# Sixteen-head gated DeltaNet trunk: the 32x32 products of the chunk inverses issued in turns instead of loop by loop

## The chip, the cores and the metric

The kernel runs on one core of one Trainium2 chip. The metric is the device time of one execution in microseconds (us); the value of a kernel is the median over its runs.

## The reference, cut to what matters

A two-layer decoder trunk over 512 tokens of width 1024: a gated DeltaNet mixer, a gated MLP with a causal convolution, sliding-window attention on a shared K/V, a second gated MLP, and a final norm. All inputs and outputs are float32. The change lies in the mixer, in what the reference writes as a triangular solve per chunk and head:

```python
m = jnp.where(strict, jnp.einsum('bnhcd,bnhsd->bnhcs', k_beta, k) * decay, 0.0)
t_mat = lax.linalg.triangular_solve(m + eye, eye, left_side=True, lower=True,
                                    unit_diagonal=True)
u = jnp.einsum('bnhcs,bnhse->bnhce', t_mat, v_beta)
w = jnp.einsum('bnhcs,bnhsd->bnhcd', t_mat, k_beta * jnp.exp(gc)[..., None])
```

`t_mat` is the inverse of a unit lower triangular matrix. The reference has chunks of 64 tokens; the kernel works with chunks of 128, which gives the same output, so each inverse is 128x128. There are 4 chunks and 16 heads, 64 inverses.

## The kernel before, in words

The mixer works in four groups of four heads. Projections run with the weights as the stationary operand: each weight block is split on ACT (`whi`, line 129) and DVE (`wlo`, line 130) into two parts, and `mm3` (lines 145 to 147) makes three matmuls of 128x128 by 128x512 per block. These "large matmuls" fill most of PE's (TensorE's) time. Their results lie in PSUM banks with the tag `d`. There are further banks with the tags `g` (two), `s` (two) and `p` (one).

A chunk's inverse is built in three steps:

- `solve` (lines 498 to 526) inverts the four 32x32 blocks on the diagonal of all 16 inverses of a group at once on DVE, by forward substitution, and sends them through DRAM into `Xg`, where they lie on the diagonal.
- `levels(g, pr)` (from line 529) fills in what is below the diagonal. It is called twice in each group, for pair 0 and pair 1 (two heads, four chunks each: 8 inverses). It first takes a transposed copy `sy` (DVE, line 532), and then has two levels. The first joins 32x32 blocks into 64x64 ones: a first stage of 32x32 products (lines 539 and 541) from `Xg` and the matrix `nt` into the banks `s` and `p`; two copies into `pz` (ACT, lines 544 and 545); and a second stage of 32x32 products (lines 548, 552 and 556) from `pz` and `sy`, read by DVE (lines 560 to 562). The second level joins 64x64 blocks: line 565, a copy on ACT (569), line 572, and DVE (580).
- `scan(g, c)` runs the recurrence over the four chunks and uses the inverses (line 610). Its output goes to DRAM (`od`), and `gate(h)` reads it back (line 674, SP's queue), scales it (ACT, 678), transposes it (PE, 681), multiplies it by the gate (DVE, 682) and stores it to `yd` (683). The output projection reads `yd` back (773), and loads and transposes `x` (784, 787).

A 32x32 product uses one 32x32 sub-array of the 128x128 array: its rows are the partitions of the operands, its columns the partitions of the result. The five loops and their sub-arrays (rows / columns): line 539, rows 0 to 31 / columns 32 to 63; line 541, 64 to 95 / 96 to 127; line 548, 32 to 63 / 32 to 63; line 552, 32 to 63 / 0 to 31; line 556, 96 to 127 / 64 to 95. Each loop makes 8 products on one and the same sub-array. A float32 product appears in the trace as two matmuls (and two weight loads).

The order of the work isn't the order of the code. The jobs of the mixer are listed in the table `ORDER`, where L0 and L1 are the two calls of `levels`, C0 to C3 the scans, `z` and `g` the gate's projections and products, and P, Q, V, K other jobs of this or the next group. Each job gets a priority from its place, and a scheduler then orders every instruction on each engine by priority and by when its inputs and its buffer are free, by its own estimate of times. So an edit in one place can move instructions elsewhere. Each engine works through its queue in order, and SP's queue issues nearly all transfers.

Of the kernel before, what the change touches and what calls it, by code (L numbers as in the profile page):

```python
# [41 lines left out]
def kernel(  # L42
# [27 lines left out]
    V, S, G, PE, SP = nc.vector, nc.scalar, nc.gpsimd, nc.tensor, nc.sync  # L70
# [36 lines left out]
    def pair(tag, dt=F32):  # L107
        return main.tile([P, 2, T], dt, tag=tag, bufs=PAIRS[tag], name=nm(tag))

    def bank(tag):  # L110
        return psum.tile([P, T], F32, tag=tag, bufs=BANKS[tag], name=nm(tag))
# [417 lines left out]
    def levels(g, pr):  # L529
        Yt = pair("sy")  # L530
        X = Xg[:, 2 * pr : 2 * pr + 2, :]
        V.transpose(Yt[:].rearrange("p h t -> p (h t)"), X.rearrange("p h t -> p (h t)"))
        y4 = Yt[:].rearrange("p h (n j) -> p (h n) j", n=NC)
        x4 = X.rearrange("p h (n j) -> p (h n) j", n=NC)
        n4 = st[g]["nt", pr][:].rearrange("p h (n j) -> p (h n) j", n=NC)
        z = pz[pr]
        p1, p2 = bank("s"), bank("p")
        for c in range(8):
            PE.matmul(p1[32:64, 32 * c : 32 * c + 32], n4[0:32, c, 32:64], x4[0:32, c, 0:32], start=True, stop=True)
        for c in range(8):  # L540
            PE.matmul(
                p2[96:128, 32 * c : 32 * c + 32], n4[64:96, c, 96:128], x4[64:96, c, 64:96], start=True, stop=True
            )
        S.copy(z[32:64, :], p1[32:64, 0:256])
        S.copy(z[96:128, :], p2[96:128, 0:256])
        p3, p4 = bank("s"), bank("p")
        for c in range(8):
            PE.matmul(
                p3[32:64, 32 * c : 32 * c + 32], y4[32:64, c, 32:64], z[32:64, 32 * c : 32 * c + 32], start=True, stop=True
            )  # L550
        for c in range(8):
            PE.matmul(
                p3[0:32, 32 * c : 32 * c + 32], z[32:64, 32 * c : 32 * c + 32], y4[32:64, c, 32:64], start=True, stop=True
            )
        for c in range(8):
            PE.matmul(
                p4[64:96, 32 * c : 32 * c + 32], z[96:128, 32 * c : 32 * c + 32], y4[96:128, c, 96:128], start=True, stop=True
            )
        blocks = lambda ps, r: ps[r : r + 32, 0:256].rearrange("p (n j) -> p n j", n=8)
        V.tensor_scalar(x4[32:64, :, 0:32], blocks(p3, 32), -1.0, None, op0=ALU.mult)  # L560
        V.tensor_scalar(y4[0:32, :, 32:64], blocks(p3, 0), -1.0, None, op0=ALU.mult)
        V.tensor_scalar(y4[64:96, :, 96:128], blocks(p4, 64), -1.0, None, op0=ALU.mult)
        p6 = bank("p")
        for c in range(8):
            PE.matmul(
                p6[64:128, 64 * c : 64 * c + 64], n4[0:64, c, 64:128], x4[0:64, c, 0:64], start=True, stop=True
            )
        p6s = tmp6
        S.copy(p6s[64:128, :], p6[64:128, :])
        p7 = bank("s")  # L570
        for c in range(8):
            PE.matmul(
                p7[0:64, 64 * c : 64 * c + 64],
                p6s[64:128, 64 * c : 64 * c + 64],
                y4[64:128, c, 64:128],
                start=True,
                stop=True,
            )
        yb = y4[0:64, :, 64:128]
        V.tensor_tensor(yb, yb, p7[0:64, :].rearrange("p (n j) -> p n j", n=8), op=ALU.subtract)  # L580
        st[g]["y", 2 * pr], st[g]["y", 2 * pr + 1] = Yt[:, 0, :], Yt[:, 1, :]
        G.memset(x4[32:64, :, 0:32], 0.0)
# [108 lines left out]
    def bias_rows():  # L691
# [20 lines left out]
        "T": key_tokens,  # L712
        "V": value_proj,
        "L": levels,
        "C": scan,
        "B": key_norms,
# [566 lines left out]
```

## Time and profile before

| what | value |
|---|---|
| median of 3 runs | 1455.04 us |
| the three runs | 1465.84, 1454.49, 1455.04 us |
| the profiled execution | 1461.97 us |
| its span (first to last instruction) | 1460.2 us |
| PE busy | 1424.7 us (98%) |
| mean granted clock of PE | 0.989 |
| the eight calls of `levels` | between 129.8 and 434.2 us |
| matmuls of each of the five 32x32 loops | 128 (8 calls x 8 products x 2) |
| first matmul of the output projection, ahead of the mixer's last scans | 441.1 us |

Durations of single matmuls overlap: PE starts one while others run, so the distance from start to start, not the duration, is what one costs. Times in the views are from the span's start. In the timeline, neighbouring instructions of one line are merged into one piece with a count; where two lines alternate, the pieces are single instructions. In the rows of stretches the columns are: stretch, length, PE busy and number of matmuls, granted clock, share of the DMA engines, GB/s.

### The profile page before, as it was taken

How to read it: one execution, taken by the hardware profiler on the slowest of the kernel's cores; microseconds unless marked ns; L12 is line 12 of the kernel's file. 1: busy time of each engine (PE TensorE's matmuls, PEld its weight loads, DVE VectorE, ACT ScalarE, POOL GpSimd, SP SyncE). 2: the span in 40 equal slices, each digit the busy share in tenths (PEclk: the TensorE clock that was granted, in tenths of full speed). 3: DMA queues.
4: the chain of work that ended last, by engine and by line, in shares of the span. 5: the costliest groups of instructions: out<-in, count | busy, mean ns of one | idle time of the engine just before them, and what ended most of it. 6: DMA issues, size and time to landing. Idle time of an engine off the chain costs nothing.

```text
span 1460.2 us, 21604 instructions
## 1 busy us (share of the span) xinstructions
PE 1424.7 (98%) x8266; PEld 1188.8 (81%) x8266; DVE 1118.9 (77%) x2048; ACT 769.7 (53%) x1510; POOL 20.0 (1%) x47
## 2 busy tenths in 40 slices
PE   7999999999999999999999999899999999999998
PEld 5778888888887788888988889777788888988887
DVE  4896885976945446888978899878667889977896
ACT  7764564655646424444434445668745444444443
POOL 1000000000000000000000000100000000000000
PEclk9999999998999999999999999999999999999999
DMA  5334253162356533231242223231033321342222
GB/s 154 83 108 111 75 175 114 62 188 73 123 163 219 161 115 108 87 116 44 96 151 87 87 60 115 87 101 51 30 114 110 99 81 60 116 137 87 94 66 79
DMA packets 163084, 152.85 MB, mean 105 GB/s; under 512 B 24164, under 2 KB 150693, under 8 KB 162981
## 3 DMA queue, kind: packets, MB, share of 16 engines
q1 hardware_dynamic: 160722, 151.27, 32.7%
q8 instruction: 65, 1.06, 0.3%
q10 hardware_dynamic: 2259, 0.20, 0.2%
q14 instruction: 38, 0.31, 0.1%
HBM read 134.65 MB, written 16.80 MB: 104 GB/s over the span
## 4 chain that ended last, share of the span: by engine, by line
PE 87%; DVE 6%; DMA 4%; ACT 2%; issue 1%; DVEq 0%; ACTq 0%; SPq 0%
PE d L145 21%; PE d L147 21%; PE d L146 21%; DVE wlo L130 2%; PE s L595 2%; PE p L1198 1%; PE s L610 1%; PE d L999 1%; PE g L1193 1%; PE s L635 1%; PE s L999 1%; PE d L997 1%; PE d L998 1%; PE s L997 1%; PE s L998 1%
## 5 line engine op out<-in xcount | busy, mean ns | idle before, releaser
L145 PE MATMUL d<-xh,whi 128*128 128x512 f32 x1192 | 476.4, 400 | 3.7 <-ACT whi L129 3.6
L147 PE MATMUL d<-xh,wlo 128*128 128x512 f32 x1192 | 475.3, 400 | 0.5 <-DVE wlo L130 0.5
L146 PE MATMUL d<-xl,whi 128*128 128x512 f32 x1192 | 474.2, 398 | 0.0
L129 ACT CAST whi<-stage 128x1024 fp32r<-128x1024 f32 (+2 forms) x236 | 229.2, 976 | 245.5 <-PE d L146 162.6
L130 DVE TENSOR_TENSOR wlo<-stage,whi 128x1024 fp32r<-128x1024 f32 (+2 forms) x236 | 265.7, 1129 | 70.2 <-ACT whi L129 69.3
L145 PEld LDWEIGHTS d<-xh,whi 128*128 128x128 f32 x1192 | 225.4, 189 | 52.1 <-ACT whi L129 4.2
L147 PEld LDWEIGHTS d<-xh,wlo 128*128 128x128 f32 x1192 | 225.5, 189 | 51.0 <-DVE wlo L130 1.4
L146 PEld LDWEIGHTS d<-xl,whi 128*128 128x128 f32 x1192 | 225.5, 189 | 48.0 <-issue 1.0
L237 DVE SCALAR_TENSOR_TENSOR acc<-d,cwc,acc 128x511 f32<-128x511 f32 (+2 forms) x96 | 70.6, 738 | 9.1 <-ACT acc L234 8.7
L858 DVE TENSOR_TENSOR sz<-d,p6s 128x512 f32<-128x512 f32 x58 | 39.9, 688 | 40.7 <-PE d L147 38.5
L880 ACT ACTIVATE dt<-dt 128x512 f32<-128x512 f32 x44 | 27.8, 632 | 82.1 <-DVE dt L863 82.1
L863 DVE SCALAR_TENSOR_TENSOR va<-sz,fcw,va 128x511 f32<-128x511 f32 (+1 forms) x58 | 43.3, 747 | 1.8 <-ACT va L861 0.9
L863 DVE SCALAR_TENSOR_TENSOR dt<-sz,fcw,dt 128x511 f32<-128x511 f32 (+1 forms) x58 | 43.3, 746 | 0.9
L517 DVE TENSOR_TENSOR sT<-sT,p6s 64x31 f32<-64x31 f32 (+15 forms) x124 | 40.8, 329 | 1.9
L511 DVE TENSOR_TENSOR p6s<-sN,sT 64x31 f32<-64x31 f32 (+15 forms) x124 | 40.8, 329 | 1.8
L129 ACT CAST whi<-st 128x768 fp32r<-128x768 f32 (+1 forms) x30 | 23.7, 791 | 29.8 <-PE g L999 6.8
L858 DVE TENSOR_TENSOR zl<-d,p6s 128x512 f32<-128x512 f32 x30 | 20.7, 689 | 23.4 <-PE d L147 22.7
L1181 ACT ACTIVATE dt<-dt,sm 128x256 f32<-128x256 f32 (+1 forms) x64 | 30.3, 473 | 6.7 <-DVE sm L1177 6.6
L882 DVE TENSOR_TENSOR va<-dt,va 128x512 f32<-128x512 f32 x44 | 30.4, 690 | 1.2
L643 ACT ACTIVATE rq<-o 128x128 f32<-128x128 f32 x64 | 19.0, 298 | 18.0 <-DVE o L638 12.4
L130 DVE TENSOR_TENSOR wlo<-st,whi 128x768 fp32r<-128x768 f32 (+1 forms) x30 | 26.8, 899 | 1.8 <-ACT whi L129 1.7
L861 ACT ACTIVATE dt<-sz,normc,fcw 128x512 f32<-128x512 f32 x29 | 23.7, 817 | 5.2 <-DVE sz L858 5.1
(745 smaller groups left out, 2814.1 us busy)
## 6 DMA issues: line engine op xcount, KB each, us to landing
stage<-in_ffn_w_up_dram SPq DMA_DIRECT2D x44, 1024.0 KB, 5.2
stage<-in_a_w_in_dram SPq DMA_DIRECT2D x23, 1024.0 KB, 5.5
stage<-in_ffn_w_down_dram SPq DMA_DIRECT2D x16, 768.0 KB, 4.6
stage<-in_a_w_out_dram SPq DMA_DIRECT2D x8, 1024.0 KB, 5.1
st<-in_ffn_w_down_dram SPq DMA_DIRECT2D x8, 768.0 KB, 5.7
zd<-sz SPq DMA_DIRECT2D x16, 256.0 KB, 2.0
od<-o SPq DMA_DIRECT2D x16, 256.0 KB, 2.6
stage<-in_b_w_q_dram SPq DMA_DIRECT2D x4, 1024.0 KB, 5.1
```

The source lines that it names most:

```text
L129: S.copy(hi[:, :kt, :m], src)
L130: V.tensor_tensor(lo[:, :kt, :m], src, hi[:, :kt, :m].bitcast(F32), op=ALU.subtract)
L145: PE.matmul(ps, hi[:, k, :m], xh[k], start=first and k == 0, stop=False)
L146: PE.matmul(ps, hi[:, k, :m], xl[k][:], start=False, stop=False)
L147: PE.matmul(ps, lo[:, k, :m], xh[k], start=False, stop=last and k == kt - 1)
L237: V.scalar_tensor_tensor(acc[:, d:], ps[:, : T - d], col, acc[:, d:], op0=ALU.mult, op1=ALU.add)
L511: V.tensor_tensor(tv, N[:, s, s + 1 : 32].unsqueeze(2).to_broadcast([64, n, m]), Tm[:, s : s + 1, 0:m].to_broadcast([64, n, m]), op=ALU.mult,)
L517: V.tensor_tensor(Tm[:, s + 1 : 32, 0:m], Tm[:, s + 1 : 32, 0:m], tv, op=ALU.subtract)
L858: V.tensor_tensor(u[:], ps[:], rs[:], op=ALU.mult)
L863: V.scalar_tensor_tensor(acc[:, d:], u[:, : T - d], tap(2 - d, t), acc[:, d:], op0=ALU.mult, op1=ALU.add)
L882: V.tensor_tensor(b[:], a[:], b[:], op=ALU.mult)
L1181: S.activation(e3[:, j, :], e3[:, j, :], AF.Exp, bias=ngm[:, j : j + 1], accum_out=den[:, j : j + 1])
```

## The change

Both loops of the first stage become one loop in which the two products of a chunk follow each other, and the three loops of the second stage become one loop with the products in the order 548, 556, 552 of the old numbering. The operands, the sub-arrays, the banks and the number of products stay as they are.

```diff
         p1, p2 = bank("s"), bank("p")
         for c in range(8):
             PE.matmul(p1[32:64, 32 * c : 32 * c + 32], n4[0:32, c, 32:64], x4[0:32, c, 0:32], start=True, stop=True)
-        for c in range(8):
             PE.matmul(
                 p2[96:128, 32 * c : 32 * c + 32], n4[64:96, c, 96:128], x4[64:96, c, 64:96], start=True, stop=True
             )
...
         p3, p4 = bank("s"), bank("p")
         for c in range(8):
-            PE.matmul(
-                p3[32:64, 32 * c : 32 * c + 32], y4[32:64, c, 32:64], z[32:64, 32 * c : 32 * c + 32], start=True, stop=True
-            )
-        for c in range(8):
-            PE.matmul(
-                p3[0:32, 32 * c : 32 * c + 32], z[32:64, 32 * c : 32 * c + 32], y4[32:64, c, 32:64], start=True, stop=True
-            )
-        for c in range(8):
-            PE.matmul(
-                p4[64:96, 32 * c : 32 * c + 32], z[96:128, 32 * c : 32 * c + 32], y4[96:128, c, 96:128], start=True, stop=True
-            )
+            ks = slice(32 * c, 32 * c + 32)
+            PE.matmul(p3[32:64, ks], y4[32:64, c, 32:64], z[32:64, ks], start=True, stop=True)
+            PE.matmul(p4[64:96, ks], z[96:128, ks], y4[96:128, c, 96:128], start=True, stop=True)
+            PE.matmul(p3[0:32, ks], z[32:64, ks], y4[32:64, c, 32:64], start=True, stop=True)
```

The line numbers of the changed kernel differ: old line 541 is 540, the copies 544 and 545 are 543 and 544, the second stage is 548 (as before), 549 (old 556) and 550 (old 552), and every later line is 8 lower (565 is 557, 674 is 666). Here is how the scheduler places the matmuls of the first call of `levels` that follow the copies, on PE. Before:

```order
L147 MATMUL d_1724<-xh_132,wlo_1726 128x512
L548 MATMUL s_907<-pz_343,sy_885 32x32 x8
L552 MATMUL s_907<-sy_885,pz_343 32x32 x8
L556 MATMUL p_908<-sy_885,pz_343 32x32 x8
L451 MATMUL g_1488<-ident_80,qT_1415 128x128
```

In these rows stand the line, the instruction, the tile that it writes, the tiles that it reads, the shape, and how often in a row. Now:

```order
L145 MATMUL d_1724<-xh_132,whi_1725 128x512
L146 MATMUL d_1724<-xl_133,whi_1725 128x512
L147 MATMUL d_1724<-xh_132,wlo_1726 128x512
L548 MATMUL s_907<-pz_343,sy_885 32x32
L549 MATMUL p_908<-sy_885,pz_343 32x32
L550 MATMUL s_907<-sy_885,pz_343 32x32
```

The last three rows come eight times. In the whole program the first stage is merged in this way in the four calls for pair 1; in the four calls for pair 0 the loops of lines 539 and 540 stand apart, with other work between them, as before. The order of the other engines' queues is the same as before in groups 0 and 1 and drifts in places in groups 2 and 3. On PE it drifts between the two stages of the last call (group 3, pair 1). Before, with L681 the gate's transposes:

```order
L541 MATMUL p_4002<-Xg,nt_3416 32x32 x8
L147 MATMUL d_4403<-xh_132,wlo_4405 128x512
L681 MATMUL g_4124<-ident_80,ol_4116 128x128
L145 MATMUL d_4403<-xh_141,whi_4404 128x512
L681 MATMUL g_4124<-ident_80,ol_4116 128x128
L146 MATMUL d_4403<-xl_142,whi_4404 128x512
L681 MATMUL g_4124<-ident_80,ol_4116 128x128
L147 MATMUL d_4403<-xh_141,wlo_4405 128x512
L681 MATMUL g_4124<-ident_80,ol_4116 128x128
L548 MATMUL s_4021<-pz_344,sy_3999 32x32 x8
```

and now

```order
L539 MATMUL s_4001<-Xg,nt_3416 32x32
L540 MATMUL p_4002<-Xg,nt_3416 32x32
L146 MATMUL d_4403<-xl_160,whi_4404 128x512
L147 MATMUL d_4403<-xh_159,wlo_4405 128x512
L548 MATMUL s_4021<-pz_344,sy_3999 32x32
L550 MATMUL s_4021<-sy_3999,pz_344 32x32
```

The transposes now stand before this call's products, and two large matmuls are left between its stages. In the calls for pair 1 of groups 0, 1 and 3 the copies of the two results come one after the other, and the scheduler starts the second stage with seven products of lines 548 and 550 before the first of line 549. At the mixer's end the order drifts on SP: before,

```order
L773 DMA zl_4536<-yd 128x512
L674 DMA dt_4322<-od 128x4x128
L674 DMA dt_4435<-od 128x4x128
L674 DMA dt_4450<-od 128x4x128
L674 DMA dt_4465<-od 128x4x128
L119 DMA stage_4749<-in_a_w_out_dram 128x8x256
```

and now

```order
L636 DMA od<-o_4276 128x512
L119 DMA stage_4749<-in_a_w_out_dram 128x8x256
L666 DMA dt_4322<-od 128x4x128
L666 DMA dt_4435<-od 128x4x128
L666 DMA dt_4450<-od 128x4x128
L666 DMA dt_4465<-od 128x4x128
```

`stage_4749` is a block of the output projection's weights, `dt_4322` to `dt_4465` are the scan's results for the last four heads, and `od<-o_4276` is the store that they read. The weights' load now stands ahead of these reads.

## The prediction

> **What bounds the kernel now.** I read the page first, then the waits of the matmul engine, then the timeline around the lines that change.
>
> ```profile
> span 1460.2 us, 21604 instructions
> PE 1424.7 (98%) x8266; PEld 1188.8 (81%) x8266; DVE 1118.9 (77%) x2048; ACT 769.7 (53%) x1510; POOL 20.0 (1%) x47
> PE 87%; DVE 6%; DMA 4%; ACT 2%; issue 1%; DVEq 0%; ACTq 0%; SPq 0%
> ```
>
> PE is busy for 98% of the span and carries 87% of the chain that ended last. So a change on PE is worth what it takes out of PE's own sequence, plus what it does to PE's few waits. In the mixer the long ones are these:
>
> ```profile
> PE g L787 <- DVE va L682: 2.8, 1, 2.8
> PE g L324 <- DVE sz L292: 2.6, 1, 2.6
> PE s L595 <- DVE S L621: 0.8, 1, 0.8
> ```
>
> No wait at a 32x32 product is among them. What those products cost is in PE's timeline; here is one second stage (three loops of eight products, group 3, pair 1). Columns: start, duration of the piece, line, count. A float32 product is two matmuls here, so a loop of eight shows as 16.
>
> ```profile
> 427.35 0.59 PE L548 MATMUL s<-pz,sy 32*32 32x32 f32 x13
> 427.75 0.21 PE L552 MATMUL s<-sy,pz 32*32 32x32 f32 x1
> 427.78 0.19 PE L548 MATMUL s<-pz,sy 32*32 32x32 f32 x1
> 427.84 0.19 PE L552 MATMUL s<-sy,pz 32*32 32x32 f32 x1
> 427.84 0.19 PE L548 MATMUL s<-pz,sy 32*32 32x32 f32 x1
> 427.87 0.48 PE L552 MATMUL s<-sy,pz 32*32 32x32 f32 x10
> 428.16 0.21 PE L556 MATMUL p<-sy,pz 32*32 32x32 f32 x1
> 428.28 0.57 PE L556 MATMUL p<-sy,pz 32*32 32x32 f32 x13
> 428.78 0.50 PE L145 MATMUL d<-xh,whi 128*128 128x512 f32 x1
> ```
>
> Two rates stand in it. One sub-array (rows by columns of the array) takes a matmul every (0.57 - 0.19)/12 = 31.7 ns. But the next loop, on another sub-array, starts 0.40 or 0.41 us after the one before: 16 x 25.3 ns, while three matmuls of the old loop are still to start (the L548 rows at 427.78 and 427.84 follow the first L552). So PE hands out a matmul every 25.3 ns, the sub-array falls behind by 6.4 ns each time, and the next sub-array isn't held up. Already today only the **last** loop of a run pays for the lag.
>
> **The change part by part.** Nothing is added or removed: the same 40 products per call, eight calls. In the rows of PE shown with the change, the three sub-arrays now take turns, where before each had its eight products in a row. This holds for all eight second stages and for the first stage of pair 1 in each group; the first stage of pair 0 (four of eight) stays in two loops far apart, since the scheduler places its halves by when their PSUM banks come free.
>
> *Second stages.* Before, the last matmul starts at 428.28 + 0.57 - 0.19 = 428.66, 1.31 us after the first. Taking turns each sub-array has three slots, 76 ns, per matmul, so none lags, and PE's hand-out sets the pace: 47 x 25.3 ns = 1.19 us. Saved 0.12 us, eight times: 0.96 us. *Merged first stages:* two loops, the last start at 16 x 25.3 + 0.021 + 15 x 31.7 = 0.90 us (0.021 for the longer first step), now 31 x 25.3 = 0.78 us: 0.12 us, four times: 0.48 us. Together **-1.4 us**. No row shows PE alternating for long, so this has bounds. Below: nothing gained, if the turns cost 2.5 ns each. Above: 25.3 ns is no limit and each sub-array runs at its own 31.7 ns, a rival below.
>
> *What waits for these products.* A merged run ends both its results at its own end, so the first of them comes later. The readers:
>
> ```profile
> 425.46 0.36 ACT L544 COPY pz<-s 32x256 f32<-32x256 f32 x1 [0.40 <-PE s L539]
> 425.87 0.36 ACT L545 COPY pz<-p 32x256 f32<-32x256 f32 x1
> ```
>
> ```profile
> 428.48 0.42 DVE L560 TENSOR_SCALAR Xg<-s 32x256 f32<-32x256 f32 x1 [2.95 <-PE s L552]
> 429.37 0.42 DVE L562 TENSOR_SCALAR sy<-p 32x256 f32<-32x256 f32 x1
> ```
>
> ```profile
> 424.74 0.59 PE L539 MATMUL s<-Xg,nt 32*32 32x32 f32 x13
> 430.37 1.14 PE L565 MATMUL p<-Xg,nt 64*64 64x64 f32 x16
> ```
>
> ```profile
> 236.21 0.50 PE L145 MATMUL d<-xh,whi 128*128 128x512 f32 x1
> 236.87 0.59 PE L548 MATMUL s<-pz,sy 32*32 32x32 f32 x13
> ```
>
> The first stage starts at 424.74. Merged, it ends 0.78 + 0.19 = 0.97 us later, so the two copies run from 1.01 to 1.37 and from 1.41 to 1.78. Where only two large matmuls stand between the stages (236.21 to 236.87, 0.66 us, in group 1), the next stage starts at 0.78 + 0.12 + 0.66 = 1.56: after the copy that L548 needs, before the end of the one that L549 needs. There the order puts seven products (0.35 us) ahead of the first L549, which makes it 1.91. Slack 0.13 us; without it the price is some 0.2 us, four times. On DVE, L560 moves from 1.13 to about 1.39 us after the second stage's start, and L562's end from 2.44 to 2.70; L565, which needs both, started 3.02 after. Other matmuls fill PE in between. I cost both moves at **nothing**, at worst 1 us together.
>
> *What the scheduler moves besides.* Queues of groups 0 and 1 keep their order but for the merged products. In groups 2 and 3 the order drifts. Between the stages in group 3, pair 1, seven rows stood before (three large matmuls and four gate transposes L681). The transposes have moved forward, and two large matmuls are left. In group 2 two became four. At the mixer's end, in SP's queue, the megabyte of weights (`stage_4749`) now goes ahead of the four reads of `dt`. That touches the chain that ends in the longest mixer wait:
>
> ```profile
> 458.94 3.05 DMA od<-o
> 462.06 3.21 DMA dt<-od
> 467.98 7.55 DMA yd<-va
> 475.54 2.60 DMA va<-zd
> 479.07 0.66 PE g L787 x4
> ```
>
> ```profile
> 466.30 0.39 SPq L119 DMA_DIRECT2D stage<-in_a_w_out_dram  x1
> ```
>
> ```profile
> yd<-zl SPq DMA_DIRECT2D x12, 256.0 KB, 3.2
> stage<-in_a_w_out_dram SPq DMA_DIRECT2D x8, 1024.0 KB, 5.1
> ```
>
> The store of `yd` took 7.55 us where its kind takes 3.2: it ran beside the weight load issued at 466.30. Now the load sits beside the reads of `dt` instead: these land at most 5.1 us later, less what of the load has moved before the first read, and the store takes up to 4.35 us less. PE's order has 65 large matmuls and 16 transposes between the last scan product and L787, now 67 and 16, which is 0.5 us more cover for the 2.84 us wait. Bounds: the whole wait goes (-2.8), or the reads lose more than the store gains (+2). I take **-1.3 us**, nearer the row with the longer overrun, since part of the load is over before the first read is issued.
>
> *Sum.*
>
> ```profile
> 234.13:237.54 3.41, 3.41 (x75) 1.00 0.12 19
> 237.54:244.37 6.83, 6.83 (x51) 0.50 0.70 202
> 329.70:333.12 3.42, 3.42 (x77) 1.00 0.27 77
> 333.12:343.36 10.24, 10.24 (x62) 0.50 0.12 19
> ```
>
> ```profile
> 240.22 0.63 PE L147 MATMUL d<-xh,wlo 128*128 128x512 f32 x1
> 240.64 0.63 PE L145 MATMUL d<-xh,whi 128*128 128x512 f32 x1
> 431.78 0.40 PE L146 MATMUL d<-xl,whi 128*128 128x512 f32 x1
> 432.02 0.39 PE L147 MATMUL d<-xh,wlo 128*128 128x512 f32 x1
> ```
>
> The profiled execution took 1461.97 us, the median of the runs shown is 1455.04. The difference has a place (stretch, length, PE busy and count, granted clock): after the small products of groups 1 and 2 the clock falls to half for 17.07 us. A large matmul then steps 0.42 to 0.43 us instead of 0.23, so about 17.07 x 0.46 = 7.9 us are lost, and 1461.97 - 7.9 = 1454.1 is what a run without these stretches should take; 1454.49 and 1455.04 are such runs by that reckoning. The terms come off either: 1461.97 - 1.4 - 1.3 = 1459.3 with the stretches, 1455.04 - 2.7 = **1452.3** without. I forecast the latter, as the median before was of that kind.
>
> **The rivals.**
>
> *The turns run side by side.* If 25.3 ns is no limit, all sub-arrays advance at 31.7 ns at once: a run of three ends after 15 x 31.7 = 0.48 us instead of 1.31, a run of two after 0.48 instead of 0.90. 8 x 0.83 + 4 x 0.42 = 8.3 us, and with the tail 1455.04 - 8.3 - 1.3 = 1445.4. For it: matmuls of two loops do overlap at each change. Against it: all three loops start exactly 25.3 ns x 16 apart, however long their queue is. The Trainium skill, TensorE: Matmul & The Clock Gate, section "Part 3: Packing small matmuls — row/col tiling", says of matmuls in different tiles that their starts lie about 4 ns apart; by it the sum would be this rival's. The same page, in the section "Wait — 56ns, not 53.3ns?", has a floor of about 25 ns from start to start; the trace agrees with that one, with 25.3, and by it the sum is my forecast.
>
> *Half clock in the median run.* Each stretch follows some 4 us with hardly any large matmul. The change shortens these by 0.24 us and gives group 2 more large matmuls, but makes such a place in group 3. If two stretches fall into the median run, it is 1452.3 + 7.9 = 1460.2. For it: the profiled execution has them. Against: two of the three timed runs, by the sum above, have not.
>
> *Every change of sub-array drains the array: slower.* Merging makes some 21 more changes in each of eight runs and 14 in each of four, 224 in all. Between the last L556 (428.66) and the large L145 (428.78) stand 0.12 us, 0.09 more than a step of 31.7 ns. At that price each: 224 x 0.09 = 20.2 us, 1455.04 + 20.2 - 1.3 = 1473.9. It decides from about 0.07 us per change. Against it: the changes from L548 to L552 to L556 go to another column and to another row of the array, and cost no gap. The Trainium skill, TensorEngine Tiling (Array Packing), section "Key Properties", has the drain when the tiling mode changes, not the tile; the trace agrees, with 0.12 us at the change of shape and none between the loops.
>
> *The turns bring nothing*, because the pace is 27.9 ns or the scheduler's drift eats it: 1455. That lies within my forecast.
>
> **How the numbers follow.** The forecast (1449 to 1456) has 0.60, the half clock 0.22, side by side 0.12, the drain 0.05, and a tail that loses several us 0.01. The range goes from 1446.5, close to the side-by-side case, to 1461.5, past the half-clock case. One per cent, 14.6 us, is about what a measurement of this kernel can tell from no change; all cases but the drain stay inside it. Faster by over 1% would need the side-by-side case and both wait and stretches gone: 0.02. Slower: the drain, 0.05. Same: 0.93.
>
> **What would show it.** Right: in a second stage the three lines alternate about 25 ns apart, the last matmul starts 1.19 us after the first, and the large one follows 0.12 us later; merged first stages span 0.78. L548 still has no wait to speak of, and L787 waits under 2.8 us. Side by side would show 0.5 us for either run; a drain, steps of 0.1 us at each change of line. I am wrong if the mixer's end (L787) moves by over 4 us in either direction while the products keep to 25 ns: then the drifted order decides, not the turns; or if more than two half-clock stretches appear.

## The result, and the profile after

The changed kernel takes 1447.04 us, the median of ten runs, the kernel before 1454.88 us, measured beside it: 7.8 us less, where I forecast 2.7 us less. Nine of the ten runs lie between 1445.78 and 1449.55 us and one, disturbed, took 3562.07. The ratio on record, which leaves that one out and is not the quotient of the medians, is 0.9932, with a 95% interval of 0.9911 to 0.9953, that is 6.8 to 12.9 us less. The profiled execution took 1446.89 us. Its page:

```profile
span 1445.1 us, 21607 instructions
PE 1407.3 (97%) x8266; PEld 1173.8 (81%) x8266; DVE 1118.4 (77%) x2048; ACT 769.7 (53%) x1510; POOL 20.0 (1%) x47
PE 85%; DVE 8%; DMA 4%; ACT 2%; issue 1%; SPq 0%; DVEq 0%; ACTq 0%
```

PE still sets the end, with the same 8266 matmuls; it is busy for 17.4 us less than in the profile of before, which had half-clock stretches that this one lacks (more on them with the second profile of before). One second stage (group 0, pair 0) in PE's timeline, from its first rows to its last and the next matmul of full size:

```profile
136.67 0.21 PE L548 MATMUL s<-pz,sy 32*32 32x32 f32 x1
136.68 0.21 PE L549 MATMUL p<-sy,pz 32*32 32x32 f32 x1
136.68 0.21 PE L550 MATMUL s<-sy,pz 32*32 32x32 f32 x1
136.72 0.19 PE L548 MATMUL s<-pz,sy 32*32 32x32 f32 x1
...
137.16 0.19 PE L548 MATMUL s<-pz,sy 32*32 32x32 f32 x1
137.17 0.19 PE L549 MATMUL p<-sy,pz 32*32 32x32 f32 x1
137.18 0.19 PE L550 MATMUL s<-sy,pz 32*32 32x32 f32 x1
137.30 0.44 PE L451 MATMUL g<-ident,qT 128*128 128x128 f32 x2
```

Three starts on three sub-arrays lie within 0.01 us (6.5 ns apart by the records behind these rows), and the whole stage goes from 136.67 to 137.18: **0.51 us** where my forecast had 1.19 and the kernel before 1.31. The next matmul, of 128x128, follows 0.12 us later, as before. Each sub-array for itself is as fast as ever: (137.16 - 136.72)/14 = 31.4 ns a step on L548. The first stage of pair 1, same view:

```profile
142.24 0.21 PE L539 MATMUL s<-Xg,nt 32*32 32x32 f32 x1
142.25 0.21 PE L540 MATMUL p<-Xg,nt 32*32 32x32 f32 x1
...
142.74 0.19 PE L540 MATMUL p<-Xg,nt 32*32 32x32 f32 x1
```

0.50 us instead of 0.90 before and 0.78 forecast. The four merged first stages all read so. Five of the eight second stages take 0.51; the other three (pair 1 of groups 0, 1 and 3, where the order has seven products of L548 and L550 ahead of the first L549) take 0.74. So the turns save 5 x 0.80 + 3 x 0.57 + 4 x 0.40 = 7.3 us. Counted from the first start of each run of small products to the next matmul that is none, all the small products of the levels took 38.0 us in a second profile of the kernel before and 30.7 now (31.0 in the expectations below).

Some of the waits of PE now:

```profile
PE p L610 <- ACT us L606: 1.6, 2, 1.2
PE g L779 <- DVE va L674: 1.4, 1, 1.4
PE g L779 <- DMA acc<-in_x_dram: 1.0, 1, 1.0
PE g L673 <- ACT ol L670: 0.9, 1, 0.9
```

L779 is the line that was L787, L610 was L618. The wait of L779 for `va`, the mixer's longest before, is down from 2.8 to 1.4 us (the one of L324 stays, 2.4 after 2.6), but three others stand beside it that were not among the long ones before. The chain through it:

```profile
448.34 2.94 DMA od<-o
451.35 5.41 DMA dt<-od
459.32 2.00 DMA yd<-va
461.34 4.55 DMA va<-zd
466.81 0.66 PE g L779 x4
```

As forecast, the read of `dt` beside the weights' load grew (3.21 to 5.41) and the store of `yd` shrank (7.55 to 2.00); the read of `zd` grew too (2.60 to 4.55), which I had not seen. The way from `od`'s issue to L779 is 18.5 us where it was 20.1.

### The profile page after: what moved, and what is told of

It is laid out like the page before. It is cut to its first block, busy times and chain, and to the rows that moved or that the text cites. A ratio compares the mean times of both kernels' runs of the same rounds, so it can differ in the third digit from the quotient of the medians.

```text
span 1445.1 us, 21607 instructions
## 1 busy us (share of the span) xinstructions
PE 1407.3 (97%) x8266; PEld 1173.8 (81%) x8266; DVE 1118.4 (77%) x2048; ACT 769.7 (53%) x1510; POOL 20.0 (1%) x47
## 4 chain that ended last, share of the span: by engine, by line
PE 85%; DVE 8%; DMA 4%; ACT 2%; issue 1%; SPq 0%; DVEq 0%; ACTq 0%
PE d L145 21%; PE d L147 21%; PE d L146 21%; DVE wlo L130 2%; PE s L587 1%; PE p L1190 1%; PE d L991 1%; PE s L627 1%; PE g L1185 1%; PE s L602 1%; PE d L989 1%; PE p L610 1%; PE s L991 1%; DVE h L994 1%; PE d L990 1%
```

## The experiments

The question was what lets the sub-arrays run side by side, in which order they must come, and what else moved the time. The times below are medians; the ratio on record is to the kernel before on the same chip, measured beside it, and is again not the quotient of the medians. The runs stand in three series, each with its own executions of the kernel before: the turns alone, blocks of four and the same rows in the first, blocks of two, both kernels once more and the joined levels in the second, the narrow weights in the third.

**The second stages' turns alone.** A second `for` keeps L539 and L540 in two loops:

```diff
             PE.matmul(p1[32:64, ...], n4[0:32, c, 32:64], x4[0:32, c, 0:32], ...)
+        for c in range(8):
             PE.matmul(p2[96:128, ...], n4[64:96, c, 96:128], x4[64:96, c, 64:96], ...)
```

> Only the second stages take turns; the two loops of the first stage stay apart, as in the kernel before. Look-ahead theory (the matmul engine lets about three matmuls that have not started wait, and starts each as soon as its own sub-array is free, 31.7 ns after that one's last): a second stage spans 0.51 us from first to last start where the three take turns from the beginning, 0.73 where the third line joins late, and the back-to-back first stage of pair 1 stays at 0.90. Eight second stages save about 5.3 us: ratio to before 0.996, some 1449.5 us. Hand-out theory (the prediction's: a matmul every 25.3 ns whatever its sub-array): a second stage spans 1.19 us, 1 us saved, 1454. Drift theory (the gain comes from the order that the scheduler moved and from missing half-clock stretches): the time falls by much more than the runs shrink, or the profile still shows half-clock stretches and the time stays near 1455.

Measured: the first stages are back at 0.90 us, the second stages take 0.51 to 0.59, and in group 3 other matmuls break them up; all small products 32.7 us. The time is 1456.49 us (1449.87 to 1459.68), the ratio 0.9984 [0.9962, 1.0006]. The products behave as under the side-by-side reading, the time does not show it: the interval holds 1. Five of the twelve executions lie at 1450 to 1454, seven at 1456 to 1460, and these have a mean granted clock of 0.989 to 0.993. What that is, is taken up with the second profile of before.

**The first stages' turns alone.** The second stage goes back to three loops:

```diff
-        for c in range(8):
-            prod_a(c); prod_b(c); prod_c(c)
+        for f in (prod_a, prod_c, prod_b):
+            for c in range(8):
+                f(c)
```

(`prod_a`, `prod_b`, `prod_c` stand for the three matmuls of L548, L549 and L550, here and below.)

> Only the first stages take turns; the second stage is three loops of eight, as before. The order of the other instructions drifts much as in the full change. Look-ahead theory: the merged first stage of pair 1 spans 0.50 us instead of 0.90, four times, 1.6 us, and the second stages stay at 1.31: 1453, ratio 0.999. Hand-out theory: 0.78, 0.5 us saved, 1454.4. Drift theory: most of the full change's 7.8 us is here too, near 1448, since the drifted order is the same.

Measured: second stages 1.31 us, merged first stages 0.50, all small products 36.4 us: 1.6 less than before. 1453.94 us, ratio 0.9978 [0.9958, 0.9998].

**Blocks of four.** The second stage in turns of four chunks instead of one:

```diff
-        for c in range(8):
-            prod_a(c); prod_b(c); prod_c(c)
+        for c0 in (0, 4):
+            for f in (prod_a, prod_b, prod_c):
+                for c in range(c0, c0 + 4):
+                    f(c)
```

> As the full change, but in the second stage each sub-array has four products (eight matmuls) before the next has its turn. Look-ahead theory with two to three waiting matmuls: a second stage spans 0.92 to 1.08 us, between the 1.31 of loops of eight and the 0.51 of single turns, since the next sub-array can only start when two or three matmuls of the block before it are left; 8 x 0.3 + 4 x 0.4 us saved, about 1451. Hand-out theory: 1.19 to 1.24 us whatever the block. A theory without a limit (every sub-array runs beside the others in any order): 0.51.

In its timeline L549, L552 and L555 are the three products:

```profile
137.17 0.34 PE L549 MATMUL s<-pz,sy 32*32 32x32 f32 x5
137.32 0.21 PE L552 MATMUL p<-sy,pz 32*32 32x32 f32 x1
137.35 0.19 PE L549 MATMUL s<-pz,sy 32*32 32x32 f32 x1
...
138.05 0.32 PE L555 MATMUL s<-sy,pz 32*32 32x32 f32 x5
```

A block is eight matmuls. L552 starts when five of L549 have started: three are still waiting for their own sub-array. The stage takes 1.01 us (0.95 where the order breaks a block), so neither a fixed hand-out of 25.3 ns (1.19) nor free sub-arrays (0.51) describes it; a limited look-ahead does. 1451.56 us, ratio 0.9946 [0.9926, 0.9967].

**Blocks of two**, the same with `c0` in (0, 2, 4, 6).

> The second stage goes in blocks of two chunks: two products of one sub-array, two of the next, two of the third, four times over; all else is the changed kernel. Look-ahead theory (a matmul of another sub-array can start while at most two or three matmuls ahead of it, in program order, have not): 0.58 to 0.65 us from first to last start, between the 0.51 of single turns and the 1.01 of blocks of four. Hand-out theory of my prediction (25.3 ns from any start to the next): 1.19 us whatever the order. No limit at all, every sub-array by itself: 0.51 us, whatever the order. Time: some 1 us above the changed kernel, within the scatter of one run.

```profile
137.32 0.21 PE L549 MATMUL s<-pz,sy 32*32 32x32 f32 x1
137.33 0.21 PE L552 MATMUL p<-sy,pz 32*32 32x32 f32 x1
137.34 0.21 PE L555 MATMUL s<-sy,pz 32*32 32x32 f32 x1
```

0.549 us, just under the range I gave, in five of the eight stages (0.76 in the other three, of which more below). The rows say why: at 137.34 the first L555 starts although three of L549 and three of L552 stand ahead of it unstarted. So the limit is not two or three matmuls in all, but three for **one** sub-array. The three starts lie 13 ns apart with four matmuls between them, 3.2 ns for a matmul. With that rule (handed out in order, every 3.2 ns, until the next one's own sub-array has three waiting; steps of 52 ns for a sub-array that had nothing waiting and of 31.7 after that) I work out 1.30 for three loops, 0.90 for two, 0.99 for blocks of four, 0.58 for blocks of two and 0.51 for single turns; measured are 1.31, 0.90, 1.01, 0.55 and 0.51, so it is close and not exact. For the three stages of the changed kernel with the L549 held back it gives 0.65 and 0.74 was measured. There something else comes in, the copy that L549 reads (two views of the changed kernel):

```profile
143.35 0.36 ACT L544 COPY pz<-p 32x256 f32<-32x256 f32 x1
143.77 0.21 PE L549 MATMUL p<-sy,pz 32*32 32x32 f32 x1
```

By the records the first L549 starts 0.05 us after this copy ends and 0.24 us after the first L548, and so it does in all three stages; the same three stages of blocks of four, of blocks of two and of the changed kernel's second profile show 0.05 to 0.06 us from copy to product too. The 0.24 and the 0.50 that sixteen matmuls of L549 take give the 0.74, so what the rule lacks here is a wait for data. The one execution took 1448.12 us.

**Two sub-arrays of the same rows.** L548 and L550 use rows 32 to 63 of the array and different columns, L549 has rows and columns of its own:

```diff
         for c in range(8):
-            prod_a(c); prod_b(c); prod_c(c)
+            prod_a(c); prod_c(c)
+        for c in range(8):
+            prod_b(c)
```

> As the full change, but in the second stage only the two products on the same rows of the array (different columns) take turns, and the third line follows as a loop of eight. Look-ahead theory: two sub-arrays that share rows run side by side too, so the pair spans 0.50 us and the whole stage about 0.95. If only sub-arrays with different rows run side by side, the pair takes turns in a row: 1.0 us for it and 1.3 to 1.4 for the stage. Hand-out theory: 1.19 to 1.29.

```profile
137.97 0.21 PE L549 MATMUL s<-pz,sy 32*32 32x32 f32 x1
137.98 0.21 PE L555 MATMUL s<-sy,pz 32*32 32x32 f32 x1
...
138.50 0.57 PE L552 MATMUL p<-sy,pz 32*32 32x32 f32 x13
```

0.91 us in all eight: the pair in the same rows runs side by side, and the loop behind it starts when three of the pair's last sub-array wait. Different columns are enough. One execution: 1452.57 us.

**Both kernels once more**, for a second profile of before and more executions of the change.

> The kernel before once more, for a second profile. Half-clock theory: the profiled execution of 1461.97 us had 17 us of half clock behind the small products of groups 1 and 2; if this one is at 1453 to 1457 us it has none there and the same products (1.31 us for each second stage, 0.90 for each merged first stage), and the difference to the changed kernel's profile, place by place, is 0.80 and 0.58 us in the second stages, 0.40 in the first. If the places of half clock are fixed by the kernel: the stretches stand at 237 and 333 us again and the time is 1462.

> The changed kernel once more, on the chip of the others. If its gain is the turns' 7.3 us: 1447 us at a mean clock of 0.996, 7 us or so below the kernel before at the same clock. If a good part of its gain was that no half-clock stretch fell behind its small products: some of its executions show a mean clock of 0.990 to 0.993 and take 1451 to 1455 us, as executions of the second stage's turns alone did.

The kernel before took 1457.68 us in this one execution, its second stages 1.31 and its merged first stages 0.90 us, and its clock is full behind the small products. But it is at half elsewhere. Stretches of this profile (length, PE busy and count, ..., granted clock), then two of the changed kernel:

```profile
472.50:475.90 3.40, 3.40 (x12) 2.70 (x11) 1.66 (x3) 1.67 (x3) 0.00 (x0) 0.50 0.82 268
745.60:749.00 3.40, 3.40 (x10) 2.62 (x9) 2.32 (x3) 2.00 (x2) 0.00 (x0) 0.50 0.00 0
```

```profile
470.00:476.00 6.00, 4.78 (x27) 3.56 (x25) 1.64 (x3) 1.89 (x4) 0.00 (x0) 1.00 0.74 221
740.00:750.00 10.00, 10.00 (x46) 8.20 (x45) 6.31 (x8) 4.35 (x6) 0.00 (x0) 1.00 0.63 207
```

So the places of half clock are not fixed: 237, 333 and 480 us in the first profile of before, 472 and 746 in the second, none of these in the changed kernel. (All three have one at 42 or 43 us, one between 905 and 920 and one at the end.) The difference between the two spans, 1455.9 - 1445.1 = 10.8 us, is 7.3 for the products and 6.8 x 0.46 = 3.1 for two stretches; the idle time of PE grew by 1.6 (36.2 to 37.8), and 2.0 of the 12.4 us of busy time that went has no place that I found.

The changed kernel took 1448.48 us (1447.67 to 1449.90), ratio 0.9944 [0.9926, 0.9963]. None of its 21 executions had a mean clock under 0.995; of 73 of the kernel before in the three series 25 had. Sorted by mean clock, the executions at 0.996 compare the kernels without the stretches, each with the kernel before of its own series:

| kernel | median at clock 0.996 (executions) | kernel before, same series | below it | small products, below before |
|---|---|---|---|---|
| changed | 1448.19 (7) | 1454.42 (7) | 6.2 | 7.3 |
| second stages' turns alone | 1450.89 (3) | 1456.68 (4) | 5.8 | 5.4 |
| blocks of four | 1451.62 (8) | 1456.68 (4) | 5.1 | 4.2 |
| first stages' turns alone | 1453.89 (3) | 1456.68 (4) | 2.8 | 1.6 |

At a like clock each of the four is below the kernel before, in the order of what its products save: the changed kernel by 1.1 us less than that, the others by 0.4 to 1.2 us more. With three to eight executions in a place, differences of that size are not resolved; that waits take back part of the changed kernel's gain, as the list above suggests, is not shown. Of the 7.0 us between the medians of its series (1455.44 and 1448.48) some 0.8 is left for half-clock stretches that it doesn't meet.

**All levels joined.** The turns carried on to the 64x64 products: both pairs of a group go through the levels together, and pair 0's lower product takes turns with pair 1's upper one.

```diff
-            PE.matmul(p1[32:64, ks], n4[0:32, c, 32:64], x4[0:32, c, 0:32], ...)
-            PE.matmul(p2[96:128, ks], n4[64:96, c, 96:128], x4[64:96, c, 64:96], ...)
-        S.copy(z[32:64, :], p1[32:64, 0:256])
-        S.copy(z[96:128, :], p2[96:128, 0:256])
-        p3, p4 = bank("s"), bank("p")
+            PE.matmul(p1[0:64, ks], n4[0:32, c, 0:64], x4[0:32, c, 0:32], ...)
+            PE.matmul(p1[64:128, ks], n4[64:96, c, 64:128], x4[64:96, c, 64:96], ...)
+        S.copy(z[0:128, :], p1[0:128, 0:256])
+        p3 = p4 = bank("p")
...
+        for c in range(8):
+            lower(p7, 0, c)
+            upper(p6, 1, c)
```

> Carries the side-by-side reading further: the two pairs of a group go through each level together. The first stage's products are made 32x64 (the other half of their columns is not used), so that both write all rows of one bank and one copy (128 partitions instead of two copies of 32) hands them on; the second stage's three lines write one bank; the 64x64 products of pair 0's lower level and pair 1's upper level take turns, in opposite corners of the array. If sub-arrays without shared rows and columns run side by side at any size: 16 + 16 starts of 64x64 in turns span 0.93 us instead of 2 x 0.92, the second stages 0.51 each, the first stages of both pairs 1.0 us instead of 1.5; the small products take about 5.8 us a group instead of 7.6, some 23 us in all against 31.0 in the changed kernel, and the time is about 1447.0 - 7.4 = 1439.6 us if large matmuls fill every wait. If 64x64 products do not overlap: the turns of 64x64 span 1.85 us and the time is about 1443.5. If the joined levels open waits that nothing fills: above 1447, with idle time in front of a line of the levels. Half-clock theory (small products in a row bring the clock down): fewer or no half-clock stretches after the levels.

Here L566 is the lower and L563 the upper product:

```profile
146.40 0.27 PE L566 MATMUL s<-sy,p6s 64*64 64x64 f32 x1
146.41 0.27 PE L563 MATMUL p<-Xg,nt 64*64 64x64 f32 x1
146.50 0.22 PE L566 MATMUL s<-sy,p6s 64*64 64x64 f32 x1
...
147.33 0.22 PE L563 MATMUL p<-Xg,nt 64*64 64x64 f32 x1
```

0.93 us for both where each alone takes 0.92: 64x64 products run side by side too. Not as expected were the first stages:

```profile
134.71 0.22 PE L546 MATMUL s<-Xg,nt 32*64 32x32 f32 x1
134.71 0.22 PE L545 MATMUL s<-Xg,nt 32*64 32x32 f32 x1
134.76 0.22 PE L546 MATMUL s<-Xg,nt 32*64 32x32 f32 x1
```

They start together, but each sub-array now steps 58 ns instead of 31.7, with the same 32 columns moved: 2.0 us for both pairs and not 1.0. The weights had become 64 columns wide. So the small products take 28.0 us in all, 2.8 less than in the changed kernel and not 8. The time is 1453.01 us, ratio 0.9972 [0.9952, 0.9991], **slower** than the changed kernel. The profiled execution is 9.8 us longer than the changed kernel's: 17 us more of half clock (7.8), PE idle for 4.4 more, less the 2.8, which places 9.4. (That execution is the slowest of its twelve.)

**Narrow weights.** Does the width of the weights alone set the step? Every 64x64 product in two of 64x32:

```diff
-            PE.matmul(p6[64:128, ...], n4[0:64, c, 64:128], x4[0:64, c, 0:64], ...)
+            for r in (64, 96):
+                PE.matmul(p6[r : r + 32, ...], n4[0:64, c, r : r + 32], x4[0:64, c, 0:64], ...)
```

and the same for the lower product with `r` in (0, 32). The first of the two kernels below also makes the copy behind L540 on DVE.

> The changed kernel with every 64x64 product split by columns into two of 64x32 (rows shared, columns apart) that take turns, and the copy behind L540 on DVE instead of ACT, which keeps large matmuls between the stages of every group. In the run with joined levels, products of 32 rows and 64 weight columns that moved 32 columns stepped 58.4 ns in their sub-array, like the 64x64 ones that move 64, and those with 32 weight columns step 31.7. If the width of the weights sets the step: a loop of eight 64x64 products (0.92 us) takes 0.50 to 0.51 us as two columns of 64x32, 16 starts of 31.7 ns each; 8 x 0.42 = 3.3 us less in the small products (about 27.7 us in all), and 1444 to 1445 us where the changed kernel takes 1447.0 to 1448.5. If the moved columns set it: 0.93 us as before and the time of the changed kernel. If one start per 25.3 ns were the limit: 32 x 25.3 = 0.81 us. If two sub-arrays in the same rows cannot run side by side: 1.0 us or more.

> The same split of the 64x64 products, with the copy behind L540 on ACT as in the changed kernel. Here the planner puts no large matmul between the stages of group 3 (after the first product of pair 0 up to pair 1's second stage), so each stage's copies and products of DVE and ACT stand open. The products take the same time as in the run beside it. If cover matters as my prediction said: idle time of PE in front of the second stages, the 64x64 products and the first stage of pair 1 in group 3, about 0.4 us per copy and 1 us per chain over DVE, 4 to 8 us together, and a time of 1449 to 1453 us. If the levels' waits are covered by something else: the time of the run beside it.

In the first of the two:

```profile
141.09 1.08 PE L558 MATMUL p<-Xg,nt 64*32 64x64 f32 x32
```

The 32 matmuls start within 1.08 - 0.21 = 0.87 us: a sub-array steps 56 ns. So the 64 columns moved keep the step as the 64 columns of weights did; of the shapes here only the product that is 32 wide in both steps 31.7. The small products gain nothing (31.0 us in all). And the time is 1460.79 us, ratio 1.0022 [1.0002, 1.0042], 12 us above the changed kernel and outside all that was expected. Waits in the profiled execution (1457.9 us of span):

```profile
PE d L145 <- ACT whi L129: 6.0, 4, 3.5
PE g L781 <- DVE va L676: 2.9, 1, 2.9
PE g L490 <- ACT va L238: 2.8, 2, 1.8
PE g L675 <- ACT ol L672: 2.2, 2, 1.6
```

None of these lines is part of the edit. The scheduler has put the other work in another order around the new products, and PE is idle for 43.5 us instead of 37.8; with 6.8 us more of half clock (3.1) and 0.3 in the products that places 9.1 of the 12.8 us. The second kernel, whose order has bare stages in group 3, took 1461.16 us, ratio 1.0024 [0.9999, 1.0048], above the 1449 to 1453 us expected. It shows what the cover was worth, in the place that I named, where PE waits 5.9 us in all; the two longest waits:

```profile
PE s L548 <- DVE sy L532: 2.8, 1, 2.8
PE p L558 <- issue: 2.0, 1, 2.0
```

but also 13.7 us of half clock, from 417.3 us on, right in these waits. Its time is like that of the other by other losses, so the two together price neither the copy on DVE nor the order.

## Why the prediction was wrong

- **The step that failed** is "PE's hand-out sets the pace: 47 x 25.3 ns = 1.19 us". The term was -1.4 us for the turns, and -7.3 was measured. The 25.3 ns were a quotient: a loop's first start follows the former loop's by 0.40 to 0.41 us, which I read as 16 hand-outs. It is the time in which 13 of the old loop's 16 matmuls start (0.052 + 11 x 0.0317 = 0.40): the next loop begins when three are left waiting. Blocks of four tell the two apart, as the next block comes after 5 of 8 there (137.17 to 137.32).
- The rows that I quoted did not decide between the two readings. Two starts at once, as at 427.84, fit both, since a matmul that was handed out early can still wait for its sub-array; and 13 starts of a loop of 16 happen to take as long as 16 hand-outs of 25.3 ns. A place of the same profile with a shorter loop does decide (group 3, pair 0, where another matmul cuts the second loop):

```profile
418.94 0.53 PE L552 MATMUL s<-sy,pz 32*32 32x32 f32 x11
419.28 0.21 PE L556 MATMUL p<-sy,pz 32*32 32x32 f32 x1
```

Here 14 matmuls of L552 stand in a row. L556 starts 0.344 us after the first of them by the records, right behind the eleventh (0.052 + 9 x 0.0317 = 0.337), with three left waiting; 14 hand-outs would be 0.354. So the 25.3 ns were no floor from start to start: they depend on the length of the loop. I had written that the loops start 16 x 25.3 ns apart "however long their queue is", and had looked at loops of one length only.

- **The rival** "the turns run side by side" was right in its mechanism and nearly in its sum: 8.3 us priced, 7.3 measured, as three stages of eight keep the L549 back for 0.23 us each and every run takes 0.50 or 0.51 us instead of 0.48. I gave it 0.12. The Trainium skill, TensorE: Matmul & The Clock Gate, section "Part 3: Packing small matmuls — row/col tiling", has starts of different tiles some 4 ns apart, and the runs here come near it, with 3.2 ns for a matmul.
- **What waits for these products** at nothing: right for DVE and the 64x64 products, which don't stand among PE's waits. Wrong for the second copy: the first L549 waits for it in three stages, 0.23 us each time. The seven products ahead of it, side by side, are no cover of 0.35 us, so the slack of 0.13 us that I had counted was not there, and the price that I had named for that case, some 0.2 us a time, was paid.
- **The tail**, -1.3 us: its transfers moved as said and the wait of L779 fell by 1.4, but L779 waits 1.0 for `acc` now and L673 0.9 for `ol`. As a gain in time it was about nothing.
- **Half clock**: the two stretches behind the small products stood in the profiled execution of before as I had them, but a third, of 3.4 us at 480 us, was not in my sum; with it the reckoning gives 1461.97 - 20.5 x 0.46 = 1452.5 and not 1454.1. The second profile of before, at 1457.68 us, has none there and two of 3.4 us elsewhere, so an execution some 3 us above the median isn't free of them; that the median has none, as I had it, was not seen in a trace. The case that I gave 0.22, two long stretches in the changed kernel, did not come.
- **Every change of sub-array drains the array** is refuted: in the turns of the changed kernel the starts on two sub-arrays in a row lie 6.5 to 18 ns apart, 39 ns once at the first round.
- A side remark in the prediction was wrong, that L540 of pair 0 stands apart until its bank comes free. In the changed kernel the four transfers into `Xg` were issued from 126.3 to 127.7 us and land 1.9 to 2.2 us later, so its data were there at 129.9, and it started at 133.3 with large matmuls up to then. Its bank was free too: no earlier instruction of the trace uses a bank `p`. The scheduler put it there; by which of its rules, no run decides.
- **Luck.** The time lies inside the range that I gave (1446.5 to 1461.5) only because I had set its lower end for the rival; the mechanism of my forecast does not reach it.

**Left open.** Why the changed kernel meets no half clock but the stretches that all profiles have, while the second stages' turns alone have a lower mean clock in over half of their executions (none of those was profiled, so the places are unknown). Shorter products don't explain it: 30.7 us of small products go with a clock of 0.996, 32.7 with 0.993 in the mean, 33.9 (blocks of four) with 0.996, 28.0 (levels joined) with 0.994. So of the change's 7.8 us the runs show the 7.3 in the products row by row; that the time of the second stages' turns alone falls with them shows only at a like clock.

## What to carry to other kernels

Before a quotient over a loop is taken for a rate, look at the rows where two loops meet: which starts first, and how many of the old loop are still to come. Small products on different parts of the array should come in turn from one product to the next, since PE takes them in order and stops while three wait for the sub-array of the next one. A gain of a few microseconds on PE is easily given back elsewhere: two kernels with equal or shorter products were 4.5 and 12 us slower than the changed one, with waits at lines that no edit had touched and with more half clock.

## What the runs showed of the hardware that was not expected

- A sub-array's step: 31.7 ns for 32x32 with 32 columns moved; 58 ns for 32x64 with 32 moved and for 64x64 with 64; 56 ns for 64x32 with 64. The first step after a pause is longer: 52 ns for 32x32, 0.10 us for 64x64 (146.40 to 146.50). In blocks of four it is 52 ns again at each new block.
- Sub-arrays in the same rows and different columns run side by side (0.91 us, two in turns and then a loop).
- About three matmuls can wait for one sub-array while those behind them go to another.
- From the end of a copy on ACT to the first start of the product that waits for it, 0.05 to 0.06 us pass (the held-back stages of four profiles).
- The granted clock falls to half for 3.4 us or two to four times that, at places that change from one execution to the next.
